# A diffusion transformer layer on one core: the modulation weights streamed at longer intervals

## The chip, the cores and the metric

The kernel runs on one core of one Trainium2 chip. A core has a matrix engine (PE, with its weight loads listed apart as PEld), a vector engine (DVE), a scalar engine (ACT), a general engine (POOL) and a sync engine (SP), which here issues transfers from device memory. Each engine works through its own list of instructions in the order in which the program wrote them. The metric is the device time of the whole program in microseconds (us), as a median of several runs.

## The reference

One transformer layer over 256 latent tokens and 256 context tokens of width 2048, all in float32. Cut to what matters here:

```python
mod = silu(c) @ w_ada + b_ada                      # 6 segments of 2048 columns
sh_a, sc_a, gt_a, sh_f, sc_f, gt_f = split(mod, 6)  # segments 0 to 5
h = rms_norm(x, g_attn) * (1 + sc_a) + sh_a        # the same for the context, from c_ctx
o = hybrid_mixer(h, hc)                            # w_in, four groups of heads, w_out
x = x + gt_a * o                                   # segment 2
h = rms_norm(x, g_ffn) * (1 + sc_f) + sh_f         # segments 4 and 3
x = x + gt_f * swiglu(h, w_g, w_u, w_d)            # segment 5; inner width 5632
out = rms_norm(x, g_final)
```

Segments 0 and 1 are needed before any projection. Segment 2 is first read at the residual of the output projection, segments 3 and 4 at the second norm, and segment 5 at the second residual.

## The kernel before

**Weights.** Every weight matrix is streamed once. `stream_w` loads two chunks of 128 rows by 512 columns (512 KB) with one transfer on SP's queue into a tile `raw` (four buffers, line 125). `split` turns each chunk into a pair: ACT rounds it (`whi`, line 137), and DVE subtracts that from the original (`wlo`, line 140). Six buffers of each hold three loads' worth of pairs. `mm3s` multiplies a pair with a pair of activations in three matmuls (lines 160, 161, 163). With 256 tokens, a load feeds twelve matmuls of 512 columns.

**Modulation columns.** Segments 2 to 5 are not done on PE. `ada_block` makes 512 columns of a segment from eight loads of 512 KB from `w_ada`, through the same four `raw` buffers. For each half of a load DVE multiplies by the conditioning value and adds into `ada_acc` (line 346; the first of the sixteen halves is ACT's, line 344). Four transposes on PE (line 351) and a reduction on DVE (line 354) finish the block. Segment 2's first half is loaded earlier, through other buffers; this is not touched.

**The order.** The program writes out the order of its instructions with a small planner, `Side`. It has a clock, `now`, in estimated microseconds of PE. The main line (projections, output projection, feed-forward) calls `side.pump(cost)` after each load's matmuls; `pump` moves the clock on and lets side tasks write their next step when it is due. The `ada_block` tasks stand in one lane, one block at a time. After each load such a task sets its next due time to the last one plus `gap`. `side.finish(tasks)` writes out whatever is left of the tasks. So `gap` decides after how many loads of the main line a load from `w_ada`, with its two DVE instructions, is put into the lists of SP and DVE.

**Stages**, by the trace before: up to 230 us the first norm and most of the projection; 230 to about 500 us the attention of three groups of heads with the rest of the projections; 500 to 612 us the output projection (`w_out`, first three quarters of its rows) beside the fourth group's attention (`diff`); to 650 us the rest of `w_out`, the second norm and the first gate columns; then the feed-forward in three groups of 4, 4 and 3 blocks of 512 inner columns. In a group all gate and up matrices (`ffn_wg`, `ffn_wu`) come first, then the down matrix (`ffn_wd`) over all the output columns. `side.finish(*gate_tasks)` stands ahead of the output projection, `side.finish(*mod_tasks)` behind its first three quarters.

**The gate rows.** `gate_rows(5, res)` turns segment 5's columns into a row on all partitions: a transpose (line 622), a copy on ACT (line 624), a transfer to device memory (line 626) and one back that spreads it (line 628), both on POOL's queue. The row is first read in the second group (line 1045); the first group only copies its sums out (`act.copy`).

Of the kernel before, what the change touches and what calls it, by code (L numbers as in the profile page):

```python
# [87 lines left out]
def hybrid_dit_kernel(ctx: ExitStack, tc: tile.TileContext, a, out):  # L88
# [31 lines left out]
    def acc():  # L120
        return psA.tile([P, 512], F32, name="acc")
# [23 lines left out]
    def stream_w(w, k0, c0, n, keep=None):  # L145
        src = w[k0 * P:(k0 + 2) * P, c0:c0 + n].rearrange("(k p) n -> p k n", p=P)
        return split(stream_raw(src, [P, 2, n]), n, keep)
# [8 lines left out]
    def mm3s(jobs, w_left=False):  # L156


        for dst, l, r, start, stop in jobs:
            pe.matmul(dst, lhsT=l[0], rhs=r[0], start=start, stop=False)  # L160
            pe.matmul(dst, lhsT=l[0 if w_left else 1], rhs=r[1 if w_left else 0], start=False, stop=False)  # L161
        for dst, l, r, start, stop in jobs:
            pe.matmul(dst, lhsT=l[1 if w_left else 0], rhs=r[0 if w_left else 1], start=False, stop=stop)  # L163

    def sub(pair, *sl):
        return pair[0][sl], pair[1][sl]
# [8 lines left out]
    def tsl(t):  # L175
        return slice(t * P, (t + 1) * P)
# [159 lines left out]
    def ada_block(seg, nb, gap, load):  # L336
        c0 = seg * D + nb * 512
        acc_ = stream.tile([P, 512], F32, name="ada_acc", bufs=2)
        for k2 in range(8):
            raw = load(ada_rows[:, 2 * k2:2 * k2 + 2, c0:c0 + 512], [P, 2, 512])  # L340
            for kk in range(2):
                kc = 2 * k2 + kk
                if kc == 0:
                    act.activation(acc_, raw[:, 0, :], AF.Copy, scale=cs[:, 0, 0:1])
                else:
                    dve.scalar_tensor_tensor(out=acc_, in0=raw[:, kk, :], scalar=cs[:, 0, kc:kc + 1], in1=acc_, op0=ALU.mult, op1=ALU.add)  # L346
            due[0] = max(due[0] + gap, side.now - 4 * gap)
            yield 0.0, max(0.0, due[0] - side.now)
        ps = misc()
        for j in range(4):  # L350
            pe.transpose(ps[:, tsl(j)], acc_[:, tsl(j)], ident)
        k4 = slice(4 * nb, 4 * nb + 4)
        base = colA1 if seg == 4 else colA
        dve.tensor_reduce(out=mcol[seg][:, k4], in_=ps.rearrange("p (j n) -> p j n", j=4), axis=AX.X, op=ALU.add)
        dve.tensor_tensor(out=mcol[seg][:, k4], in0=mcol[seg][:, k4], in1=base[:, seg * 16 + 4 * nb:seg * 16 + 4 * nb + 4], op=ALU.add)
        if seg == 4:
            dve.tensor_tensor(out=mcol[4][:, k4], in0=mcol[4][:, k4], in1=colB[:, 16 + 4 * nb:20 + 4 * nb], op=ALU.mult)
        yield 0.3, 0.0

    def add_ada(seg, gap, load, nbs=range(4)):  # L360
        due[0] = side.now
        return [side.add(ada_block(seg, nb, gap, load), lane="gate", width=1) for nb in nbs]
# [256 lines left out]
    def gate_rows(seg, pool_):  # L619

        ps = misc()
        pe.transpose(ps[0:16, 0:P], mcol[seg], ident)
        gr = small.tile([16, P], F32, name="gr", bufs=1)
        act.copy(gr, ps[0:16, 0:P])
        gd = dram.tile([D], F32, name=f"gd{seg}")
        pool.dma_start(gd.rearrange("(n p) -> n p", p=P), gr)
        g = pool_.tile([P, D], F32, name="gate")
        pool.dma_start(g, gd.partition_broadcast(P))
        return g

    GAP = 2.6
    gate_tasks = add_ada(2, GAP, stream_raw, (2, 3))
    mod_tasks = add_ada(4, GAP, stream_raw) + add_ada(3, GAP, stream_raw)

# [359 lines left out]
    def gu(w, fb):  # L994
        accs = [acc() for _ in range(2)]
        for k2 in range(0, KC, 2):
            w_ = stream_w(w, k2, fb * 512, 512)
            mm3s([j for t in range(2) for j in gu_jobs(accs[t], w_, k2, t)])
            side.pump(2.6)
        return accs  # L1000

    def act_T(sg, ps, pair, t):
        dve.tensor_tensor(out=sg, in0=ps, in1=sg, op=ALU.mult)
        yield 0.0, 1.5
        transposes_ff(pair, sg, t)
        yield 0.43, 0.0
# [7 lines left out]
        dve.tensor_tensor(out=pair[1][:, :, tsl(t)], in0=v, in1=pair[0][:, :, tsl(t)].bitcast(F32), op=ALU.subtract)  # L1014

    groups = [(0, 4), (4, 8), (8, 11)]
    gate_f = add_ada(5, 4.0, stream_raw)
    gfin = ff.tile([P, D], F32, name="gfin")
    pool.dma_start(gfin, a["g_final"].partition_broadcast(P))
    for gi, (f0, f1) in enumerate(groups):  # L1020
        last = gi == len(groups) - 1
        aT, tasks = {}, {}
        for fb in range(f0, f1):
            ga = gu(a["ffn_wg"], fb) if fb else first_g
            sg = []
            for t in range(2):
                s_ = ff.tile([P, 512], F32, name="sg", bufs=4)
                act.activation(s_, ga[t], AF.Silu)
                sg.append(s_)
            ua = gu(a["ffn_wu"], fb)  # L1030
            aT[fb] = (ff.tile([P, 4, S], F32R, name="ah", bufs=6), ff.tile([P, 4, S], F32R, name="al", bufs=6))
            tasks[fb] = [side.add(act_T(sg[t], ua[t], aT[fb], t), lane="e", width=4) for t in range(2)]
        if gi == 0:
            side.finish(*gate_f)
            gtf = gate_rows(5, res)
        def down_jobs(ps, w_, fb, j, t):
            return [(ps, sub(aT[fb], slice(None), jj, tsl(t)), w_[jj - j], fb == f0 and jj == 0, fb == f1 - 1 and jj == 3) for jj in (j, j + 1)]

        def down_evac(ps, nb, t):
            c = slice(nb * 512, (nb + 1) * 512)  # L1040
            if gi == 0:
                act.copy(y[nb][:, t, :], ps)
            elif not last:
                dve.tensor_tensor(out=y[nb][:, t, :], in0=ps, in1=y[nb][:, t, :], op=ALU.add)
                dve.tensor_tensor(out=y[nb][:, t, :], in0=y[nb][:, t, :], in1=gtf[:, c], op=ALU.mult)
                dve.tensor_tensor(out=x2[:, t, c], in0=x2[:, t, c], in1=y[nb][:, t, :], op=ALU.add)
            else:
                dve.tensor_tensor(out=y[nb][:, t, :], in0=ps, in1=gtf[:, c], op=ALU.mult)
                dve.tensor_tensor(out=x2[:, t, c], in0=x2[:, t, c], in1=y[nb][:, t, :], op=ALU.add)
                act.activation(y[nb][:, t, :], x2[:, t, c], AF.Square, accum_out=ss3[:, t, nb:nb + 1])  # L1050
                if nb < 3:
                    dve.tensor_tensor(out=x2[:, t, c], in0=x2[:, t, c], in1=gfin[:, c], op=ALU.mult)

        for nb in range(4 - last):
            accs = [acc() for _ in range(2)]
            for fb in range(f0, f1):
                side.finish(*tasks[fb])
                for j in (0, 2):
                    w_ = stream_w(a["ffn_wd"], fb * 4 + j, nb * 512, 512)
                    mm3s([q for t in range(2) for q in down_jobs(accs[t], w_, fb, j, t)])  # L1060
                    side.pump(2.6)
            for t in range(2):
                down_evac(accs[t], nb, t)
# [92 lines left out]
```

## Time and profile before

| | |
|---|---|
| median of 3 runs | 1394.29 us (1393.55 to 1402.66) |
| profiled execution | 1398.19 us |
| its span in the trace | 1396.4 us |
| PE busy | 1356.3 us, 97% |
| weight loads busy (PEld) | 1080.1 us, 77% |
| DVE busy | 913.2 us, 65% |
| ACT busy | 619.1 us, 44% |
| moved from device memory | 310.36 MB, 224 GB/s over the span |

Busy time of PE is modelled: matmuls overlap their successors, so a stretch with short gaps can still read as fully busy. The granted clock of PE was 0.994 of full speed over the span. The 16 DMA engines' busy share is a mean.

### The profile page before, as it was taken

What the parts mean: (1) busy time and instruction counts of PE and PEld (TensorE: products, weight loads), DVE (VectorE), ACT (ScalarE), POOL (GpSimd) and SP (SyncE); (2) the same over time, 40 slices, a digit from 0 to 9 for tenths busy, and PEclk for the clock granted to TensorE, in tenths of its full rate; (3) what the DMA queues carried; (4) which work ended last, traced back from release to release, by engine and by line L of the source; (5) the groups of instructions that cost most, each with busy time, mean ns of one, the idle gap of its engine ahead of it and who ended that gap; (6) DMA issues with size and microseconds to landing.
All of it is one profiled execution on the core that took longest, in us unless ns stands there. A gap on an engine that the chain in (4) does not pass through costs nothing.

```text
span 1396.4 us, 19886 instructions
## 1 busy us (share of the span) xinstructions
PE 1356.3 (97%) x7082; PEld 1080.1 (77%) x7082; DVE 913.2 (65%) x1623; ACT 619.1 (44%) x1180; POOL 34.6 (2%) x46
## 2 busy tenths in 40 slices
PE   6999999999999999999999999999999999999997
PEld 4766778767886687777877788888888888888886
DVE  3555679988887827769667765445455565555575
ACT  4522223455333626548443454444444444444443
POOL 1010000100000000000000000000000000000000
PEclk9999999999999999999999999999999999999999
DMA  9998896667888736455878876666666656666654
GB/s 337 329 313 281 279 314 213 200 223 248 282 257 293 236 102 203 147 159 182 277 270 287 284 257 217 192 196 195 186 190 187 191 176 209 193 192 186 191 173 144
DMA packets 183607, 313.78 MB, mean 225 GB/s; under 512 B 14002, under 2 KB 53972, under 8 KB 182356
## 3 DMA queue, kind: packets, MB, share of 16 engines
q1 hardware_dynamic: 179104, 302.03, 67.8%
q0 software_dynamic: 1056, 7.36, 1.4%
q10 hardware_dynamic: 3348, 3.13, 0.7%
q8 instruction: 55, 0.90, 0.2%
q14 instruction: 44, 0.36, 0.1%
HBM read 310.36 MB, written 2.11 MB: 224 GB/s over the span
## 4 chain that ended last, share of the span: by engine, by line
PE 77%; DMA 11%; DVE 6%; ACT 2%; issue 2%; POOL 0%; ACTq 0%; SPq 0%; POOLq 0%; DVEq 0%
PE acc L160 24%; PE acc L161 23%; PE acc L163 23%; DMA raw<-in_w_ada_dram 5%; PE m L270 2%; DVE wlo L140 2%; DVE ada_acc L346 2%; DMA raw<-in_w_in_dram 2%; DMA araw<-in_w_ada_dram 1%; DMA raw<-in_ffn_wg_dram 1%; DMA raw<-in_ffn_wu_dram 1%; ACT whi L137 1%; PE m L601 1%; PE m L550 1%; PE m L839 1%
## 5 line engine op out<-in xcount | busy, mean ns | idle before, releaser
L140 DVE TENSOR_TENSOR wlo<-raw,whi 128x512 fp32r<-128x512 f32 (+1 forms) x764 | 491.0, 681 | 336.0 <-ACT whi L137 323.0
L137 ACT CAST whi<-raw 128x512 fp32r<-128x512 f32 (+1 forms) x764 | 433.3, 615 | 601.9 <-PE acc L161 398.8
L160 PE MATMUL acc<-whi,h_hi 128*128 128x512 f32 x704 | 276.6, 393 | 4.2 <-ACT whi L137 4.0
L161 PE MATMUL acc<-whi,h_lo 128*128 128x512 f32 x704 | 274.3, 390 | 0.0
L163 PE MATMUL acc<-wlo,h_hi 128*128 128x512 f32 x704 | 191.8, 391 | 1.6 <-DVE wlo L140 1.4
L346 DVE SCALAR_TENSOR_TENSOR ada_acc<-raw,cs,ada_acc 128x512 f32<-128x512 f32 x210 | 156.8, 747 | 37.0 <-DMA raw<-in_w_ada_dram 31.0
L160 PE MATMUL acc<-whi,h 128*128 128x512 f32 (+1 forms) x416 | 167.4, 405 | 2.7 <-DVE ropet L569 1.6
L160 PEld LDWEIGHTS acc<-whi,h_hi 128*128 128x128 f32 x704 | 132.1, 188 | 36.0 <-ACT whi L137 9.5
L161 PE MATMUL acc<-whi,h 128*128 128x512 f32 (+1 forms) x416 | 158.2, 382 | 0.0
L163 PEld LDWEIGHTS acc<-wlo,h_hi 128*128 128x128 f32 x704 | 131.8, 188 | 31.3 <-DVE wlo L140 4.1
L161 PEld LDWEIGHTS acc<-whi,h_lo 128*128 128x128 f32 x704 | 132.2, 188 | 26.7 <-DVE h_lo L956 0.2
L160 PE MATMUL acc<-whi,ah 128*128 128x512 f32 (+1 forms) x364 | 138.9, 383 | 0.0
L161 PE MATMUL acc<-whi,al 128*128 128x512 f32 (+1 forms) x364 | 138.6, 382 | 0.0
L163 PE MATMUL acc<-wlo,h 128*128 128x512 f32 (+1 forms) x416 | 114.9, 381 | 0.2 <-DVE wlo L140 0.2
L160 PEld LDWEIGHTS acc<-whi,h 128*128 128x128 f32 x416 | 78.4, 189 | 27.6 <-issue 10.5
L163 PE MATMUL acc<-wlo,ah 128*128 128x512 f32 (+1 forms) x364 | 96.2, 382 | 0.0
L163 PEld LDWEIGHTS acc<-wlo,h 128*128 128x128 f32 x416 | 76.6, 189 | 15.7 <-DVE wlo L140 1.2
L161 PEld LDWEIGHTS acc<-whi,h 128*128 128x128 f32 x416 | 78.7, 189 | 12.9 <-issue 1.4
L160 PEld LDWEIGHTS acc<-whi,ah 128*128 128x128 f32 x364 | 68.4, 188 | 13.3
L161 PEld LDWEIGHTS acc<-whi,al 128*128 128x128 f32 x364 | 68.4, 188 | 13.2
L163 PEld LDWEIGHTS acc<-wlo,ah 128*128 128x128 f32 x364 | 67.6, 188 | 13.3
L160 PE MATMUL acc<-whi,o_hi 128*128 128x512 f32 x128 | 51.4, 402 | 0.0
(228 smaller groups left out, 1275.7 us busy)
## 6 DMA issues: line engine op xcount, KB each, us to landing
raw<-in_w_ada_dram SPq DMA_DIRECT2D x112, 512.0 KB, 4.5
raw<-in_ffn_wg_dram SPq DMA_DIRECT2D x88, 512.0 KB, 4.2
raw<-in_ffn_wu_dram SPq DMA_DIRECT2D x88, 512.0 KB, 4.3
raw<-in_ffn_wd_dram SPq DMA_DIRECT2D x88, 512.0 KB, 4.6
raw<-in_w_in_dram SPq DMA_DIRECT2D x72, 512.0 KB, 5.0
araw<-in_w_ada_dram SPq DMA_DIRECT2D x128, 256.0 KB, 4.7
raw<-in_w_out_dram SPq DMA_DIRECT2D x32, 512.0 KB, 3.8
araw<-in_w_ada_dram SPq DMA_DIRECT2D x16, 512.0 KB, 5.4
```

Of the source, the lines that this page charges most:

```text
L137: act.copy(hi, raw[:, k])
L140: dve.tensor_tensor(out=lo, in0=raw[:, k], in1=hi.bitcast(F32), op=ALU.subtract)
L160: pe.matmul(dst, lhsT=l[0], rhs=r[0], start=start, stop=False)
L161: pe.matmul(dst, lhsT=l[0 if w_left else 1], rhs=r[1 if w_left else 0], start=False, stop=False)
L163: pe.matmul(dst, lhsT=l[1 if w_left else 0], rhs=r[0 if w_left else 1], start=False, stop=stop)
L270: pe.matmul(mv[32 * j:32 * j + 32, :P], lhsT=cs32[:, kc, :], rhs=raw[:, kk, j // 2, tsl(j % 2)], start=(kc == 0), stop=(kc == KC - 1), ski ...
L346: dve.scalar_tensor_tensor(out=acc_, in0=raw[:, kk, :], scalar=cs[:, 0, kc:kc + 1], in1=acc_, op0=ALU.mult, op1=ALU.add)
L550: pe.transpose(ps[:, tsl(j)], src[:, tsl(j)], ident)
L601: pe.matmul(o[:, :S], lhsT=vt(kc)[:, v0:v0 + P], rhs=pT[:, kc, :], start=(kc == 0), stop=(kc == 3))
L839: pe.matmul(sc, lhsT=df_qT[hb, h, tsl(t)], rhs=df_kT[h // 2][hb, h % 2, :], start=True, stop=True)
```

## The change

Two intervals grow and one point moves. Segments 2 (second half), 4 and 3, ten blocks with 80 loads, are planned one load per 3.6 units of the planner's clock in place of 2.6. Segment 5, four blocks with 32 loads, is planned one per 8.0 in place of 4.0. The `finish` of segment 5 and its `gate_rows` move from the first group of the feed-forward to the second, to the same place in it: behind the gate and up matrices, ahead of the down matrix.

```diff
-    GAP = 2.6
+    GAP = 3.6
     gate_tasks = add_ada(2, GAP, stream_raw, (2, 3))
     mod_tasks = add_ada(4, GAP, stream_raw) + add_ada(3, GAP, stream_raw)
...
-    gate_f = add_ada(5, 4.0, stream_raw)
+    gate_f = add_ada(5, 8.0, stream_raw)
...
-        if gi == 0:
+        if gi == 1:
             side.finish(*gate_f)
             gtf = gate_rows(5, res)
```

No instruction is added or removed; DVE, ACT and PE have as many of each kind as before. What it does to the order is seen at three places. The numbers behind a tile's name only tell one tile from another.

SP's list at the first up matrix of the feed-forward, before:

```order
L125 DMA raw_6721<-in_ffn_wu_dram 128x2x512
L125 DMA raw_6744<-in_w_ada_dram 128x2x512
L125 DMA raw_6748<-in_ffn_wu_dram 128x2x512
L125 DMA raw_6770<-in_w_ada_dram 128x2x512
L125 DMA raw_6774<-in_ffn_wu_dram 128x2x512
L125 DMA raw_6796<-in_ffn_wu_dram 128x2x512
L125 DMA raw_6818<-in_w_ada_dram 128x2x512
L125 DMA raw_6822<-in_ffn_wu_dram 128x2x512
L125 DMA raw_6844<-in_w_ada_dram 128x2x512
```

The same place now:

```order
L125 DMA raw_6721<-in_ffn_wu_dram 128x2x512
L125 DMA raw_6744<-in_w_ada_dram 128x2x512
L125 DMA raw_6748<-in_ffn_wu_dram 128x2x512
L125 DMA raw_6770<-in_ffn_wu_dram 128x2x512
L125 DMA raw_6792<-in_ffn_wu_dram 128x2x512
L125 DMA raw_6814<-in_w_ada_dram 128x2x512
L125 DMA raw_6818<-in_ffn_wu_dram 128x2x512
L125 DMA raw_6840<-in_ffn_wu_dram 128x2x512
L125 DMA raw_6862<-in_ffn_wu_dram 128x2x512
```

Between the first and the last load of segment 5 stood 44 weight loads in SP's list before, with one or two between neighbours; now it is 94, mostly three between neighbours, and the loads reach through the first group's down matrix into the second group's first gate matrix.

SP's list where the projections end and the output projection begins, before:

```order
L125 DMA raw_5210<-in_w_in_dram 128x2x512
L125 DMA raw_5244<-in_w_in_dram 128x2x512
L125 DMA raw_5316<-in_w_out_dram 128x2x512
L125 DMA raw_5368<-in_w_out_dram 128x2x512
L125 DMA raw_5398<-in_w_out_dram 128x2x512
L125 DMA raw_5420<-in_w_out_dram 128x2x512
```

The same place now:

```order
L125 DMA raw_5157<-in_w_in_dram 128x2x512
L125 DMA raw_5189<-in_w_ada_dram 128x2x512
L125 DMA raw_5241<-in_w_out_dram 128x2x512
L125 DMA raw_5263<-in_w_ada_dram 128x2x512
L125 DMA raw_5297<-in_w_out_dram 128x2x512
L125 DMA raw_5319<-in_w_ada_dram 128x2x512
L125 DMA raw_5331<-in_w_ada_dram 128x2x512
L125 DMA raw_5335<-in_w_out_dram 128x2x512
L125 DMA raw_5357<-in_w_out_dram 128x2x512
```

Before, the last load of the 80 stood five loads ahead of the first `w_out` load. Now 15 of the 80 stand behind it, among 14 of the 24 `w_out` loads of that stage; the other ten have none.

DVE's list in the same stage, behind the first residual (lines 898 and 899; lines 845 to 847 and 859 belong to `diff`), before:

```order
L899 TENSOR_TENSOR x_5286<-x_5286,tm 128x512
L846 TENSOR_SCALAR p<-p,l_5530 128x512
L140 TENSOR_TENSOR wlo<-raw,whi 128x512
L847 SCALAR_TENSOR_TENSOR p<-p,st 128x512
L140 TENSOR_TENSOR wlo<-raw,whi 128x512 x7
L859 TENSOR_REDUCE ss<-ropet 128x2
```

The same place now:

```order
L899 TENSOR_TENSOR x_5211<-x_5211,tm 128x512
L846 TENSOR_SCALAR p<-p,l_5479 128x512
L354 TENSOR_REDUCE mcol_317<-m 128x4
L847 SCALAR_TENSOR_TENSOR p<-p,st 128x512
L355 TENSOR_TENSOR mcol_317<-mcol_317,colA 128x4
L140 TENSOR_TENSOR wlo<-raw,whi 128x512 x4
L346 SCALAR_TENSOR_TENSOR ada_acc<-raw,cs,ada_acc 128x512 x5
L859 TENSOR_REDUCE ss<-ropet 128x2
```

The multiply-adds of the modulation now stand between the weights' subtractions and the softmax work of the fourth group of heads, where there were none.

## Rows read from the trace of the kernel before

**Rows 1.** The page, part 1: busy time, share of the span, count.

```profile
PE 1356.3 (97%) x7082; PEld 1080.1 (77%) x7082; DVE 913.2 (65%) x1623; ACT 619.1 (44%) x1180; POOL 34.6 (2%) x46
```

**Rows 2.** Windows: busy us and instructions of each engine in four stretches.

```profile
core 0: us, PE busy (x) PEld busy (x) DVE busy (x) ACT busy (x) POOL busy (x), PEclk, DMA share, GB/s
230.00:500.00 270.00, 259.00 (x1245) 202.44 (x1244) 225.60 (x444) 118.25 (x260) 12.81 (x12) 0.99 0.74 239
500.00:650.00 150.00, 148.44 (x691) 115.66 (x689) 106.59 (x208) 82.31 (x170) 5.29 (x9) 1.00 0.48 157
650.00:810.00 160.00, 154.00 (x682) 121.56 (x682) 120.13 (x194) 71.86 (x129) 1.39 (x2) 1.00 0.82 274
1000.00:1160.00 160.00, 160.00 (x719) 132.72 (x718) 89.15 (x140) 70.94 (x126) 0.00 (x0) 1.00 0.63 190
```

**Rows 3.** Windows of line 346 alone: DVE busy us (count), the same stretches.

```profile
230.00:500.00 270.00, 111.91 (x150) 0.99 0.74 239
500.00:650.00 150.00, 0.00 (x0) 1.00 0.48 157
650.00:810.00 160.00, 44.90 (x60) 1.00 0.82 274
```

**Rows 4.** Waits of weight loads, 650 to 810 us: total us, times, longest.

```profile
PEld acc L160 <- ACT whi L137: 9.5, 18, 1.8
PEld acc L163 <- DVE wlo L140: 3.8, 7, 1.7
```

**Rows 5.** Waits of SP's queue, 650 to 810 us.

```profile
SPq L125 <- DVE wlo L140: 90.2, 51, 5.8
SPq L125 <- DVE ada_acc L346: 25.1, 31, 2.4
```

**Rows 6.** Waits of DVE, 650 to 810 us.

```profile
DVE ada_acc L346 <- DMA raw<-in_w_ada_dram: 21.1, 16, 4.3
DVE wlo L140 <- ACT whi L137: 13.7, 15, 1.8
```

**Rows 7.** The chain that ended last, 850 to 880 us: start us, us.

```profile
860.33 0.91 PE acc L163 x4
863.04 0.91 PE acc L163 x4
865.76 0.91 PE acc L163 x4
```

**Rows 8.** The page, part 5: busy us, mean ns of one.

```profile
L140 DVE TENSOR_TENSOR wlo<-raw,whi 128x512 fp32r<-128x512 f32 (+1 forms) x764 | 491.0, 681 | 336.0 <-ACT whi L137 323.0
L346 DVE SCALAR_TENSOR_TENSOR ada_acc<-raw,cs,ada_acc 128x512 f32<-128x512 f32 x210 | 156.8, 747 | 37.0 <-DMA raw<-in_w_ada_dram 31.0
```

**Rows 9.** The page, part 6: KB of a load, median us to landing.

```profile
raw<-in_w_ada_dram SPq DMA_DIRECT2D x112, 512.0 KB, 4.5
```

**Rows 10.** Waits of PE's matmuls, 230 to 500 us.

```profile
PE m L607 <- ACT p L579: 1.8, 1, 1.8
PE m L550 <- DVE mcol L355: 1.6, 1, 1.6
PE acc L160 <- DVE ropet L569: 1.6, 1, 1.6
PE m L692 <- ACT p L579: 1.3, 1, 1.3
```

**Rows 11.** Waits of weight loads, 500 to 650 us.

```profile
PEld acc L163 <- DVE wlo L140: 3.4, 8, 1.1
PEld m L839 <- ACT p L579: 1.0, 1, 1.0
```

**Rows 12.** Timeline of POOL, 815 to 850 us: start, us, instruction, idle before.

```profile
836.37 0.51 POOL L626 DMA_DIRECT2D gd<-gr  x1 [166.45 <-ACT gr L624]
839.42 0.55 POOL L628 DMA_DIRECT2D gate<-gd  x1 [2.55 <-DMA gd<-gr]
```

**Rows 13.** Line 628 alone: us to landing of its two transfers.

```profile
DMA to landing us min/median/max: 7.1/7.8/8.6
```

**Rows 14.** Timeline of DVE, 1118 to 1128 us: the gate row's first use.

```profile
1124.06 1.28 DVE L1045 TENSOR_TENSOR y<-y,gate 128x512 f32<-128x512 f32 x2
```

## The prediction

> **What bounds the kernel now.** I read the page's first part first: PE is busy for 97% of the span, DVE for 65%, ACT for 44% [rows 1]. So PE sets the time, and a change that adds and removes no instruction can only win or lose where PE waits. The windows show where that is [rows 2]. From 1000 to 1160 us PE is busy for all 160 us. In the chain that ended last, the fourth matmul group of one load of weights follows that of the load before by 2.72 us (863.04 - 860.33) [rows 7]; this is PE's own pace when nothing stops it, with DVE busy for only 89 of 160 us. Three stretches are short of it: 11.0 us of idle PE from 230 to 500 us, 1.6 us from 500 to 650 us, 6.0 us from 650 to 810 us.
>
> Next, what those stretches have in common. The modulation's multiply-adds (line 346) take 111.9 us of DVE in the first stretch, none in the second and 44.9 us in the third [rows 3]. DVE is busy for 84%, 71% and 75% of them (225.60 of 270, 106.59 of 150, 120.13 of 160). The queue waits of the third stretch tell the mechanism. SP waits 90.2 us for DVE's subtraction and 25.1 us for the multiply-add to free one of the four `raw` buffers [rows 5]; DVE waits 21.1 us for loads of `w_ada` to land and 13.7 us for ACT's rounding [rows 6]; and weight loads of PE wait 9.5 us for the rounding and 3.8 us for the subtraction [rows 4]. A ring of four buffers is turning slower than PE eats.
>
> **Part 1, the feed-forward (interval 4 to 8).** First what is lost there now. From below: 719 matmuls took 160 us undisturbed, 0.2225 us each, so the 682 of the third stretch are worth 151.8 us, and 8.2 us are lost. This is low, since the stretch holds part of the second norm's transposes, which are shorter. From above: the two waits together, 13.3 us, some of which may pass under a running matmul. I take the middle, 10.75 us.
>
> On how to read that loss, the rows give two answers: PE reads 6.0 us idle, while its weight loads read 121.56 us busy against 132.72 us in the undisturbed stretch, which is 13.5 us short when scaled to 160 us [rows 2]. The Trainium skill, in Perfetto Trace Analysis, Identifying the Most-Contended Engine, calls matmul busy time a poor measure and the busy share of weight loads a good one; by it this part would be worth 13.5 us, by matmul busy time 6.0 us. The waits above lie at 13.3 us and the count at 8.2 us, so the trace leans to the page's measure without settling it.
>
> Next, what is left of it. SP's list has 44 weight loads between the first and last of segment 5 before, and 94 now, mostly three to one. Four buffers turn once per four loads. With three weights to one `w_ada`, that is 3 x 2.72 = 8.2 us of PE's time; with the denser pattern before (28 to 44) it is 4 x 44/72 x 2.72 = 6.7 us. A landing takes 4.5 us [rows 9], two multiply-adds 1.5 us and two subtractions 1.3 to 1.4 us [rows 8], 7.3 us if they come one behind the other. So the ring was short by 0.6 us a turn, and now has 0.9 us to spare. DVE's own work per turn is 3 x 1.36 + 1.49 = 5.6 us of the 8.2. The loads now lie under the gate, up and down matrices up to the second group, where DVE had 44% of its time free [rows 2]: two multiply-adds per three loads fill 1.5 of 8.2 us. I leave 0.75 us of waits for blocks' ends (transposes, the first half on ACT) and take a gain of **10 us**, ends 5 and 13.3.
>
> **Part 2, attention (interval 2.6 to 3.6).** Of the 80 loads, 15 are now behind the first load of `w_out`: 30 multiply-adds of 0.747 us, 22.4 us of DVE [rows 8]. From 230 to 500 us DVE falls from 225.6 to 203.2 us, 84% to 75%. What PE waits for there is mostly not weights but the softmax and rope chains: 1.8 and 1.3 us for an exponential before scores, 1.6 us for a modulation column, 1.6 us for a rope [rows 10]. These chains pass through DVE's list, behind the multiply-adds, so a shorter list brings them forward. No row shows this stretch at 75%. I take a slope from its neighbour, which has the same kind of work: 4.1 us of idle PE per 100 us at 84%, 1.0 us at 71%, so 0.24 per point. Nine points over 270 us are a gain of **6 us**. Ends: 0, if the chains wait on ACT and PE alone, and 11.0, all the idle there is.
>
> **Part 3, the output projection.** The same 22.4 us arrive in the second stretch: 106.6 becomes 129.0 of 150 us, 86%. By the same slope 15 points over 150 us cost **5 us**. Ends: 0, if it fits into DVE's 43 idle us, and 22.4 us, every moved instruction exposed. I stay low because PE has a lead there: pairs for three loads, and with `diff` between them a load takes PE longer than 2.72 us. Weight loads already wait 3.4 us for subtractions in that stretch [rows 11], so it is not free. Segments 3 and 4 are still done ahead of the second norm: the last of their loads stands before 18 loads of `w_out`.
>
> **Part 4, the gate row.** Its chain moves from the first group's down matrix to the second's, and so loses its long slack. Before, from the start of its first transfer to the latest landing of its second it took 839.42 + 8.6 - 836.37 = 11.7 us [rows 12, 13]. Its first reader comes eight loads behind the same place in the program, 8 x 2.72 = 21.8 us; in the trace that reader started at 1124.06 us [rows 14]. So 10 us of cover are left, and I cost it at **nothing**. If the transfers queued as badly as to double, DVE would wait 2 us, in front of the subtractions of the next weights. POOL has nothing else queued behind it but the last norms.
>
> **Sum.** -10 - 6 + 5 + 0 = -11 us. The profiled execution took 1398.19 us, so it would be about 1387 us; it is 3.9 us above the median of 1394.29 us, which I use for the forecast: **1383 us**, 0.8% faster.
>
> **The rivals.** A change of 1% (14 us, below 1380.3 or above 1408.2 us) is about what a measurement of this kernel can tell from none.
>
> *Both relieved.* If PE's lead covers the output projection's extra work whole (part 3 at about 1) and attention gains 8, with 11 in the feed-forward, the sum is -18: 1376 us. For it: the second stretch has 43 us of idle DVE; in attention the busy measure hides short gaps, as it does in the third stretch (6.0 read, 8.2 to 13.3 lost). Against it: 86% is more than attention has now, and that loses 4%.
>
> *A toll per load.* Each `w_ada` load might cost PE the same wherever it stands: it takes one of four buffers and two DVE slots ahead of the next weight. Then the feed-forward's 10.75 us, 0.34 us for each of 32 loads, are spread and not removed, and parts 2 and 3 cancel: about -2, 1392 us. For it: SP waits on buffers all through [rows 5]. Against it: a stall needs the ring to run dry, and three pairs in hand (8.2 us) outlast one landing of 4.5 us. The Trainium skill's Perfetto Trace Analysis, Roofline, bears on this rival: it puts a single core's ceiling at 16 transfer engines' 435 GB/s, far above the 274 GB/s of that stretch, so by it bandwidth was not scarce and spacing the loads frees none.
>
> *The output projection becomes DVE's.* The fourth group's softmax, the subtractions and the multiply-adds share one list in order. If that list falls behind for good, the moved 22.4 us show almost whole: +20 there, -6 in attention, -10 in the feed-forward: +4, 1398 us. It decides for slower once a moved microsecond costs more than 0.7 (16 of 22.4). For it: the multiply-adds come in runs of up to five there, 3.7 us ahead of a `diff` reduction. Against it: attention at 84% lost 11 us of 270 with 112 us of them.
>
> *It does not do what it says.* Were the loads bunched at a `finish`, PE would stand still; the order shows none there, so this is worth 2%, about 1396 us.
>
> **Chances.** Forecast (1380 to 1388) 0.42; both relieved 0.33; toll 0.15; output projection 0.08; bunched or a late gate row 0.02. The forecast's own range is 1378 to 1388 us. The range for 8 in 10 takes in most of both neighbours: 1372 to 1393 us. Faster by over 1% gets the whole of "both relieved" and the low edge of the forecast, 0.39; slower by over 1% needs more than the output projection's case, 0.03; the rest, 0.58, is within 1%.
>
> **What would show it.** Right: in the feed-forward's first gate and up matrices after, weight loads wait under 2 us in place of 13.3, PE's matmuls come at 2.72 us a load, and DVE's wait for landings of `w_ada` is near zero. In attention the waits for exponentials shrink; from 500 to 650 us DVE is busy for some 129 us and weight loads wait longer than 3.4 us for subtractions. The gate row's reader waits for PE, not for a landing. Wrong: waits of the same size in the feed-forward spread over twice the length (toll); a PE idle of 10 us or more between 500 and 650 us (output projection); a wait for `gate` in the second group.

## The result, and the profile after

The change made the kernel slower: 1412.36 us (median of 6 runs, 1408.12 to 1414.63) against 1395.84 us before on the same chip (6 runs, 1392.59 to 1402.66), a ratio of 1.011 with a 95% interval of 1.0085 to 1.0135. The forecast was 1383 us, at most 1393. Single executions of one kernel lie up to 0.5% to either side of its median, and each stage below is read from one execution. Pairs of kernels whose lists are the same up to the feed-forward, or in it, show how far such a reading can be trusted (the labels are those of the experiments): 4.3 us apart at the end of attention (before_ordered, hold_26), 2.5 us in the output projection (gap_only, after), 4.7 us in the first gate and up matrices (before, gap_only), 3.9 us in the first down matrix (after, gate_only).

First the head of the page of after: span, and busy time of each engine. It answers to [rows 1].

```profile
span 1411.3 us, 19892 instructions
PE 1358.8 (96%) x7082; PEld 1080.9 (77%) x7082; DVE 909.5 (64%) x1623; ACT 618.3 (44%) x1180; POOL 34.6 (2%) x46
```

The work is the same; 15 us of waiting came in. Where, the windows of after tell; the first three and the last answer to [rows 2].

```profile
core 0: us, PE busy (x) PEld busy (x) DVE busy (x) ACT busy (x) POOL busy (x), PEclk, DMA share, GB/s
230.00:500.00 270.00, 257.35 (x1247) 202.66 (x1246) 205.57 (x412) 117.14 (x259) 12.17 (x12) 1.00 0.66 207
500.00:650.00 150.00, 141.12 (x647) 108.81 (x646) 116.03 (x220) 74.97 (x152) 5.89 (x8) 0.98 0.64 209
650.00:810.00 160.00, 158.54 (x714) 129.16 (x713) 107.87 (x181) 79.04 (x147) 1.44 (x2) 1.00 0.70 230
820.00:980.00 160.00, 153.00 (x658) 121.04 (x658) 92.69 (x150) 67.88 (x121) 0.00 (x0) 1.00 0.70 228
1000.00:1160.00 160.00, 160.00 (x720) 132.62 (x719) 85.38 (x134) 72.66 (x129) 1.06 (x2) 1.00 0.66 196
...
```

The first gate and up matrices gained (158.54 us of PE against 154.00), attention did not (257.35 against 259.00), the output projection lost (141.12 against 148.44). A stretch that was full before, 820 to 980 us, has 153.00 of 160 us: the first down matrix. Fixed windows cut through stages that shift, so the table gives each stage's length, from its first matmul to the next stage's, read from PE's timeline ("attention" from 230 us).

| us | attention | output projection, norm | first gate, up | first down | second gate, up |
|---|---|---|---|---|---|
| before | 299.9 | 113.5 | 192.2 | 88.1 | 176.8 |
| after | 297.8 | 125.3 | 183.9 | 99.5 | 178.7 |
| difference | -2.1 | +11.8 | -8.3 | +11.4 | +1.9 |

They sum to +14.7 us, the spans' difference being 14.9. Attention's -2.1 us lies within the spread just named; the three large differences lie outside it. The page's costliest groups name a suspect; the last numbers are the engine's idle time ahead of these instructions, and what ended most of it. The second row answers to the one of line 346 in [rows 8].

```profile
L140 DVE TENSOR_TENSOR wlo<-raw,whi 128x512 fp32r<-128x512 f32 (+1 forms) x764 | 487.9, 680 | 236.7 <-ACT whi L137 225.7
...
L346 DVE SCALAR_TENSOR_TENSOR ada_acc<-raw,cs,ada_acc 128x512 f32<-128x512 f32 x210 | 157.2, 749 | 155.5 <-DMA raw<-in_w_ada_dram 138.3
```

DVE stood still for 138.3 us until a load of `w_ada` landed, 31.0 us before. The forecast had this wait near zero. By stretch, DVE's waits in attention, in the first gate and up matrices (with [rows 6] before) and around the first down matrix:

```profile
DVE ada_acc L346 <- DMA raw<-in_w_ada_dram: 34.7, 28, 3.5
```

```profile
DVE ada_acc L346 <- DMA raw<-in_w_ada_dram: 41.8, 14, 4.4
DVE wlo L140 <- ACT whi L137: 5.6, 4, 2.8
```

```profile
DVE ada_acc L346 <- DMA raw<-in_w_ada_dram: 43.1, 12, 5.0
```

Before, the same wait in attention was 9.9 us, and around the first down matrix, where no `w_ada` load stood, none. Now the first down matrix close up. DVE's timeline of after, each row a run of like instructions, in brackets the idle time before it and what ended that:

```profile
865.61 1.54 DVE L346 SCALAR_TENSOR_TENSOR ada_acc<-raw,cs,ada_acc 128x512 f32<-128x512 f32 x2 [4.96 <-DMA raw<-in_w_ada_dram]
867.07 3.69 DVE L140 TENSOR_TENSOR wlo<-raw,whi 128x512 fp32r<-128x512 f32 x6
874.86 1.54 DVE L346 SCALAR_TENSOR_TENSOR ada_acc<-raw,cs,ada_acc 128x512 f32<-128x512 f32 x2 [4.09 <-DMA raw<-in_w_ada_dram]
876.31 3.70 DVE L140 TENSOR_TENSOR wlo<-raw,whi 128x512 fp32r<-128x512 f32 x6
...
893.96 0.75 DVE L346 SCALAR_TENSOR_TENSOR ada_acc<-raw,cs,ada_acc 128x512 f32<-128x512 f32 x1 [4.93 <-DMA raw<-in_w_ada_dram]
```

SP's timeline of the same place, its issues of loads:

```profile
869.59 0.37 SPq L125 DMA_DIRECT2D raw<-in_w_ada_dram  x1
870.79 7.21 SPq L125 DMA_DIRECT2D raw<-in_ffn_wd_dram  x3
878.83 0.37 SPq L125 DMA_DIRECT2D raw<-in_w_ada_dram  x1
880.04 6.98 SPq L125 DMA_DIRECT2D raw<-in_ffn_wd_dram  x3
```

A load of `w_ada` is issued at 869.59 us. DVE comes to its multiply-adds at 870.76 (867.07 + 3.69) and stands there to 874.86, when it lands. Then six subtractions of three loads follow without a pause: two of those loads had been issued before that of `w_ada`, and ACT had rounded both by 874.4 us (it began at 871.16 and 873.24 us). Only these subtractions free their buffers for SP's next loads. So the ring turns in (893.96 - 865.61)/3 = 9.45 us; PE needs 3 x 2.72 = 8.16 us for its three loads. ACT, starved in turn, waits for the down matrix, and PE's weight loads for the subtraction (both 830 to 960 us):

```profile
ACT whi L137 <- DMA raw<-in_ffn_wd_dram: 51.1, 24, 4.4
```

```profile
PEld acc L163 <- DVE wlo L140: 14.4, 20, 1.7
```

DVE's list as built says why. The numbers behind `raw` grow in the order in which the loads are issued; 8472 is a load of `w_ada`, the others are of the down matrix.

```
L140 TENSOR_TENSOR wlo_8414<-raw_8406,whi_8412 128x512
L346 SCALAR_TENSOR_TENSOR ada_acc_7957<-raw_8472,cs_113,ada_acc_7957 128x512 x2
L140 TENSOR_TENSOR wlo_8432<-raw_8428,whi_8430 128x512
L140 TENSOR_TENSOR wlo_8436<-raw_8428,whi_8434 128x512
L140 TENSOR_TENSOR wlo_8454<-raw_8450,whi_8452 128x512
L140 TENSOR_TENSOR wlo_8458<-raw_8450,whi_8456 128x512
```

The multiply-adds of 8472 stand ahead of the subtractions of 8428 and 8450, which were loaded before. In the program's text they come behind: SP's list of loads is in the text's order, DVE's is not. So what the opening section says of the engines' lists, that they are in the order in which the program wrote them, does not hold for DVE. Counted over the lists, a `w_ada` load overtakes at least one older load of weights 25 times of 112 before (8 ahead of the first load of `w_out`, 17 in the feed-forward) and 78 times of 112 after (42 ahead of the first load of `w_out`, 5 among those of `w_out`, 31 in the feed-forward, there by 1.6 loads in the mean against 0.6).

### The profile page after: what moved, and what is told of

It reads as the page before. It is cut to its first block, busy times and chain, and to the rows that moved or that the text cites. A ratio compares the mean times of both kernels' runs of the same rounds, so it can differ in the third digit from the quotient of the medians.

```text
span 1411.3 us, 19892 instructions
## 1 busy us (share of the span) xinstructions
PE 1358.8 (96%) x7082; PEld 1080.9 (77%) x7082; DVE 909.5 (64%) x1623; ACT 618.3 (44%) x1180; POOL 34.6 (2%) x46
## 4 chain that ended last, share of the span: by engine, by line
PE 50%; DMA 7%; DVE 6%; issue 1%; ACT 1%; POOL 0%; DVEq 0%; POOLq 0%; ACTq 0%
PE acc L163 16%; PE acc L160 16%; PE acc L161 16%; DVE wlo L140 3%; DMA raw<-in_w_ada_dram 3%; DMA raw<-in_ffn_wg_dram 2%; DMA raw<-in_ffn_wd_dram 1%; DMA raw<-in_w_out_dram 1%; DVE ada_acc L346 1%; PE m L1011 1%; PE m L855 0%; DMA raw<-in_ffn_wu_dram 0%; ACT whi L137 0%; DVE tm L898 0%; DVE st L577 0%
## 5 line engine op out<-in xcount | busy, mean ns | idle before, releaser
L346 DVE SCALAR_TENSOR_TENSOR ada_acc<-raw,cs,ada_acc 128x512 f32<-128x512 f32 x210 | 157.2, 749 | 155.5 <-DMA raw<-in_w_ada_dram 138.3
L163 PE MATMUL acc<-wlo,ah 128*128 128x512 f32 (+1 forms) x364 | 99.7, 388 | 6.2 <-DVE wlo L140 5.3
L160 PEld LDWEIGHTS acc<-whi,ah 128*128 128x128 f32 x364 | 68.4, 188 | 13.5
```

## Experiments

The theory that these runs were to test, "order": the intervals are harmless, and the overtakings that came with them cost the time. Its rivals: the ring of four buffers is too short for the new spacing; a `w_ada` load costs what it costs wherever it stands; DVE has too much to do.

**The parts alone.** One kernel has only the interval of 3.6, one only the change to segment 5:

```diff
 gap_only                                       gate_only
-    gate_f = add_ada(5, 8.0, stream_raw)      -    GAP = 3.6
+    gate_f = add_ada(5, 4.0, stream_raw)      +    GAP = 2.6
-        if gi == 1:
+        if gi == 0:
```

> Only the first interval is changed (2.6 to 3.6), the feed-forward stays as before. If the losses of the two parts are independent, attention gains 2 us, the output projection loses 12 us and the feed-forward is as before: 1405 us against 1396. If the loss in the feed-forward of the changed kernel came from a late start of that stage, some of it shows here too and the time is above 1408.

> Only segment 5's interval and its finish are changed (4 to 8, second group). Independent parts: first gate and up matrices 8 us shorter, first down matrix 11 us longer, 2 us at the start of the second group: about 1401 us. If the down matrix loses only because the output projection came late, it loses nothing here and the time is 1388.

The first took 1402.61 us (ratio 1.0047, 1.0025 to 1.0068), the second 1402.08 us (1.0034, 1.0014 to 1.0053). Both parts lose, 6.0 and 5.5 us against 1396.62 us before in the same runs; together that is 11.5 of the change's 16.5 us, each of these figures being uncertain by some 3 us. The stages (table below) put the loss of the first into the output projection, that of the second into the first down matrix; each takes back some of it in its own stretch. (The profiled executions show less of the losses, spans of 1397.3 and 1398.0 us against 1396.4: they lie 3.5 and 2.3 us below their kernels' medians, that of before 1.6 us above the 1396.62 us.) The wait for landings of `w_ada` is longer in both than before, but it does not go by the number of overtakings alone: 63.8 us with 64 of them in the first, 98.4 us with 39, all but 8 in the feed-forward, in the second.

**The order alone.** SP's list stays as it is after the change. DVE's multiply-adds, and the first half on ACT, are held behind the rounding and the subtraction that were written last before them; `newest` holds these, and `after` is the kernel's own helper for it. The same was done to the kernel before.

```diff
+                with (after(newest["act"], newest["dve"]) if load is stream_raw else ExitStack()):
                     if kc == 0:
                         act.activation(acc_, raw[:, 0, :], AF.Copy, scale=cs[:, 0, 0:1])
                     else:
                         dve.scalar_tensor_tensor(...)
```

> The changed kernel, with each multiply-add of the modulation held behind the newest weight's subtraction in DVE's list; SP's list is the same. Theory order (DVE's list puts the multiply-adds ahead of subtractions of weights that were asked for earlier, so DVE stands still for a landing with landed weights behind it): DVE's wait for landings of w_ada falls from 138 us to under 80, the first down matrix from 99 us to under 93, total 1398 to 1403. Theory ring (one w_ada in four loads fills four buffers with a turn longer than PE's pace, whatever DVE's order): the down matrix stays at 97 us or more and the total within 4 us of 1412.

> The kernel before, with the same hold. In its DVE list the hold removes 25 overtakings but also puts most multiply-adds of attention earlier than the planner had them. Theory order, if only overtaking counts: 1390 to 1396. Theory cover (what counts is how much DVE work stands between the moment a buffer is free and the multiply-add on what is loaded into it): attention worse, DVE's wait for landings from 31 us to over 60, 1400 or more.

After, held: 1390.48 us, ratio 0.9943 (0.9922 to 0.9965), so the slowdown of 1.1% becomes a gain of 0.6%; "order" had forecast only 1398 to 1403 us. Before, held: 1392.62 us, 0.9971 (0.9954 to 0.9989). The group of the multiply-adds on the page of after held:

```profile
L347 DVE SCALAR_TENSOR_TENSOR ada_acc<-raw,cs,ada_acc 128x512 f32<-128x512 f32 x210 | 157.2, 750 | 10.6 <-DMA raw<-in_w_ada_dram 6.3
```

6.3 us of waiting in place of 138.3, with the same loads in the same order on SP and the same work on DVE. In the feed-forward PE's list is the same too, and of ACT's only three first halves of blocks moved, so there the order alone was tested. In attention and the output projection the hold also moved instructions in PE's and ACT's lists; what it gained there may be in part theirs. DVE's timeline in its first down matrix:

```profile
857.42 1.53 DVE L347 SCALAR_TENSOR_TENSOR ada_acc<-raw,cs,ada_acc 128x512 f32<-128x512 f32 x2
858.93 1.29 DVE L140 TENSOR_TENSOR wlo<-raw,whi 128x512 fp32r<-128x512 f32 x2
861.65 1.29 DVE L140 TENSOR_TENSOR wlo<-raw,whi 128x512 fp32r<-128x512 f32 x2 [1.43 <-ACT whi L137]
864.37 1.29 DVE L140 TENSOR_TENSOR wlo<-raw,whi 128x512 fp32r<-128x512 f32 x2 [1.43 <-ACT whi L137]
865.58 0.75 DVE L347 SCALAR_TENSOR_TENSOR ada_acc<-raw,cs,ada_acc 128x512 f32<-128x512 f32 x1
```

The subtractions come at PE's pace, 2.72 us apart, the multiply-adds fit between them without a wait, and the turn is 865.58 - 857.42 = 8.16 us. Its windows:

```profile
230.00:500.00 270.00, 264.28 (x1275) 209.37 (x1275) 206.47 (x412) 119.58 (x261) 9.10 (x12) 0.99 0.64 207
500.00:650.00 150.00, 144.03 (x659) 109.95 (x658) 124.14 (x239) 81.26 (x169) 5.95 (x8) 0.99 0.65 214
650.00:810.00 160.00, 159.75 (x726) 131.67 (x726) 109.96 (x180) 78.64 (x141) 1.45 (x2) 1.00 0.77 250
820.00:980.00 160.00, 160.00 (x719) 132.67 (x718) 98.49 (x153) 73.42 (x131) 0.00 (x0) 1.00 0.73 236
```

Attention and the feed-forward are now better than before; the output projection still has 6 us of idle PE. That remainder is a second cause.

**A fifth buffer.** Room for it comes from two padding tiles. Once with the list held, once on the change as it is (shown is one of the two lines that name the number of buffers):

```diff
-        raw = stream.tile(shape, F32, name="raw", tag="raw", bufs=4)
+        raw = stream.tile(shape, F32, name="raw", tag="raw", bufs=5)
```

> after_ordered with five raw buffers in place of four (two padding tiles left out to make room). If what the output projection still loses (15 us of idle PE against 7 before) comes from loads that are late, idle PE there falls to 9 us or less, total 1384 or less. If it comes from DVE's own work, the total stays within 3 us of after_ordered's 1390.5.

> The change with a fifth buffer for raw (two padding tiles left out for the room) and no hold on the list. As built, its DVE list has no multiply-add of the feed-forward ahead of the subtractions of weights loaded earlier, while in attention and the output projection 35 of 80 still are. Theory that the order costs the time: the first down stage falls from 99.5 us to 88 to 90 us, the first gate and up from 183.9 to 181 to 183 us, the output projection stays at 120 to 126 us; in all 1391 to 1399 us. Rival, that loads of w_ada under the down matrix cost the time through the transfers: the down stage stays above 95 us and the time above 1403 us.

Held: 1384.54 us, 0.9906 (0.9878 to 0.9935), but not for the reason given: the output projection stayed at 123.2 us, and what was gained lies in attention. Not held: 1400.62 us, 1.0026 (1.001 to 1.0043). The second expectation failed for the down stage: 98.4 us, not 88 to 90. Its premise was a miscount. Counted by load, this list has 85 overtakings of 112, more than the change's 78, and in the down stage a `w_ada` load stands ahead of 2.7 older ones in place of 1.7: with one buffer more the list was built with its multiply-adds further ahead. So the pair is a test of order after all. With five buffers in both, the first down matrix takes 88.5 us held and 98.4 us not held. The wait on the page of the one not held:

```profile
L344 DVE SCALAR_TENSOR_TENSOR ada_acc<-raw,cs,ada_acc 128x512 f32<-128x512 f32 x210 | 157.4, 750 | 144.6 <-DMA raw<-in_w_ada_dram 121.1
```

A fifth buffer does not remove the wait, so a ring that is merely too short is not the cause. In attention it helps either way, by 5 to 6 us, not much more than the 4.3 us by which like lists differ there.

**The output projection: how many loads.** The held list with intervals of 2.6 and 3.0 (segment 5 as changed), which leave none and one of the `w_ada` loads behind the first load of `w_out` in place of 15 (by SP's list as built, where 79 and 65 of the 80 lie ahead; the expectation below has 77 and 64):

```diff
-    GAP = 3.6
+    GAP = 2.6        (3.0 in the other)
```

> Hold as in after_ordered, segment 5 at 8 with the finish in the second group, but segments 2, 4 and 3 at 2.6 again. Theory order: with DVE's list held, the longer interval of segment 5 alone is worth what before_ordered still loses in the first gate and up matrices (6 us of idle PE against under 2): 1387 to 1389. Theory ring: three weights to one w_ada is no better than before_ordered: 1392 or more.

> The same at an interval of 3.0: 77 of the 80 loads lie ahead of the output projection in place of 64. If attention and the output projection trade DVE time one for one, 1388 to 1391, as at 2.6 and 3.6. If the output projection pays more for a multiply-add than attention does, idle PE there is 7 to 9 us in place of 15 with attention at 20 to 24, and the time is 1383 to 1387.

1385.82 us, 0.9917 (0.989 to 0.9943), and 1382.5 us, 0.9894 (0.9865 to 0.9923). Both are a little below the ranges that were expected for "order" and for an output projection that pays more for a load than attention does. Both bring the output projection back to 114 us (before 113.5) and keep the feed-forward's gain.

**The output projection: work or loads.** Three kernels, all held at 3.6. The first leaves out every second multiply-add of segments 3 and 4. The second leaves out the multiply-adds of the loads that stand between the output projection's, and keeps the loads; the third leaves out those loads and keeps the multiply-adds, which read one resident tile instead. `in_out` is true from the first load of `w_out` to `side.finish(*mod_tasks)`.

```diff
 hold_half
+                if kk == 1 and seg in (3, 4):
+                    continue
 w_out_noadd
-                    if kc == 0:
+                    if in_out[0] and kc:
+                        pass
+                    elif kc == 0:
 w_out_noload
-            raw = load(ada_rows[:, 2 * k2:2 * k2 + 2, c0:c0 + 512], [P, 2, 512])
+            raw = held if in_out[0] else load(ada_rows[:, 2 * k2:2 * k2 + 2, c0:c0 + 512], [P, 2, 512])
```

> after_ordered, but every second multiply-add of segments 3 and 4 is left out (64 of 150, so the columns are not those of the reference); all loads stay. If the output projection's and attention's remaining losses are DVE's work, idle PE in the output projection falls from 15 us to 8 to 10, in attention from 19 to 12 to 16, total 1378 to 1385. If they come from the loads, both stay, 1389 or more.

> This is the change with the list held (multiply-adds of w_ada stay behind the subtractions of the newest weights), and in the first three quarters of the output projection the 14 or 15 loads of w_ada are still issued and land, but their multiply-adds on DVE are left out. The stretch from the first matmul of the output projection to the first of the feed-forward's first gate took 122.9 us with the held list at 3.6 and 114.1 us at 3.0. Theory that the loads themselves do it (they sit in the four buffers between the loads of w_out, so that weights come late and ACT waits for them, 17.4 us there against none before): the stretch stays at 120 to 125 us, ACT still waits over 8 us for landings of w_out. Theory that DVE's work or its place in the list does it: 113 to 116 us and no such wait.

> The same kernel as the change with the list held, but in the first three quarters of the output projection the w_ada loads are left out and the multiply-adds, all still there, read one tile that is already in memory. Theory that the loads do it: the stretch falls from 122.9 us to 113 to 116 us, ACT's wait for landings of w_out goes from 17.4 us to under 3. Theory that DVE's work or its place does it: 120 us or more stays, with PE waiting for p or mcol of DVE.

1389.35 us (ratio 0.9939, 0.9917 to 0.9961), 1392.5 us (0.9968, 0.9953 to 0.9983) and 1384.51 us (0.9911, 0.9893 to 0.9929). With half or none of the multiply-adds there the stage stays at 124.9 and 125.8 us; without the loads it falls from 122.9 to 117.0 us, a little short of the 113 to 116 expected. (Its attention ends 3.7 us later than after_ordered's, which is within the spread of like lists.) ACT's wait for landings of `w_out`, 500 to 612 us, in after held, in the kernel without the multiply-adds, and what ACT waits for most in the one without the loads:

```profile
ACT whi L137 <- DMA raw<-in_w_out_dram: 17.4, 6, 5.2
```

```profile
ACT whi L135 <- DMA raw<-in_w_out_dram: 17.3, 4, 9.5
```

```profile
ACT whi L135 <- PE acc L159: 26.4, 14, 4.3
```

Without the loads, and before, ACT has no wait for `w_out` and waits for PE instead, which is as it should be. So the loads of `w_ada` among those of `w_out` cost some 6 of the 9 us by which the held stage is longer than before, give or take the spread of 2.5 us, and the work of DVE alone is not seen to cost any. (PE's granted clock has a part in these lengths; see the last section.) In the kernel without the multiply-adds one path can be followed. ACT's timeline, then PE's:

```profile
540.85 1.14 ACT L135 CAST whi<-raw 128x512 fp32r<-128x512 f32 x2 [9.51 <-DMA raw<-in_w_out_dram]
542.41 0.72 ACT L346 ACTIVATE ada_acc<-raw,cs 128x512 f32<-128x512 f32 x1 [0.43 <-DMA raw<-in_w_ada_dram]
543.04 1.05 ACT L555 COPY pT<-m 128x512 f32<-128x512 f32 x2
```

```profile
533.75 0.71 PE L552 MATMUL m<-ident,p 128*128 128x128 f32 x5
...
543.66 2.56 PE L841 MATMUL m<-df_kT,qT 64*128 64x512 f32 x4 [5.40 <-ACT pT L555]
```

ACT stood 9.51 us for a load of `w_out`, with the copies for `diff` (line 555) behind it in its list, though PE had finished the transposes that they copy by 534.5 us; PE stood 5.40 us for the copies. It is the same fault on another engine: ready work behind an instruction that waits for a landing.

**The fastest tried.** Interval 3.0, held, five buffers:

> The held list at interval 3.0 with a fifth buffer, the candidate for the fastest. At 3.6 the fifth buffer shortened attention from 291.9 to 289.5 us and the output projection from 122.9 to 121.8 us. If buffers limit attention here too: attention 292 to 295 us in place of 296.2 us, 1378 to 1382 us. If not: 1382 to 1384 us, as with four.

1382.03 us, 0.9889 (0.9869 to 0.9909). Attention took 292.2 us in place of 296.4, the output projection 112.7 in place of 114.1, the first gate and up 182.6 in place of 180.7. That is not to be told from hold_30 with four buffers; both beat the kernel before and the change. (For the 289.5 and 121.8 us that the expectation quotes for five buffers at 3.6, the trace has 286.5 and 123.2, and for 291.9 and 296.2 it has 291.7 and 296.4.)

The stages of the profiled executions, us, with the time that DVE waited for landings of `w_ada`:

| | attention | output projection, norm | first gate, up | first down | second gate, up | wait |
|---|---|---|---|---|---|---|
| gap_only | 296.2 | 122.8 | 187.5 | 88.1 | 176.8 | 63.8 |
| gate_only | 299.1 | 113.5 | 185.6 | 95.6 | 178.0 | 98.4 |
| after_ordered | 291.7 | 122.9 | 180.8 | 88.4 | 177.3 | 6.3 |
| before_ordered | 300.9 | 113.6 | 186.5 | 88.1 | 176.8 | 7.9 |
| hold36_raw5 | 286.5 | 123.2 | 182.7 | 88.5 | 177.3 | 2.5 |
| after_raw5 | 291.9 | 119.3 | 186.6 | 98.4 | 178.0 | 121.1 |
| hold_26 | 296.6 | 113.7 | 180.7 | 88.4 | 177.3 | 6.5 |
| hold_30 | 296.4 | 114.1 | 180.7 | 88.4 | 177.3 | 7.5 |
| hold_half | 289.8 | 124.9 | 180.7 | 88.4 | 177.3 | 15.6 |
| w_out_noadd | 291.1 | 125.8 | 180.7 | 88.4 | 177.3 | 2.3 |
| w_out_noload | 295.4 | 117.0 | 180.7 | 88.4 | 177.3 | 3.9 |
| hold30_raw5 | 292.2 | 112.7 | 182.6 | 88.5 | 177.3 | 2.8 |

## Why the prediction was wrong

By stages the sum came out some 26 us too low: 15 us in part 1, 4 in part 2, 7 in part 3.

**The step that failed** is the ring turn of part 1: "Four buffers turn once per four loads ... 7.3 us if they come one behind the other. So the ring was short by 0.6 us a turn, and now has 0.9 us to spare." The loads' spacing was read from SP's list, and DVE's instructions were taken to stand in the same order. They do not. With a multiply-add ahead of two older loads' subtractions, the landing of the youngest load is added to the turn while older loads lie landed behind it: 9.45 us measured, where 7.3 had been worked out and PE allows 8.16. The rows to see it were there. DVE's 21.1 us of waits for landings of `w_ada` [rows 6] were read as a ring that runs dry; before_ordered shows that the overtakings made most of that wait (over the whole program 7.9 us in place of 31.0, and a median 4.0 us lower). A smaller slip in the same step: SP's list has 46 weight loads to the 32 of segment 5 before, and 93 after, not 44 to 28 and 94; the turn that PE allowed before was 4 x 46/78 x 2.72 = 6.4 us, not 6.7.

**Part 1.** The gain in the first gate and up matrices came, 8.3 us of the 10 (3.6 us against gap_only, whose feed-forward has the list of before and took 187.5 us there); "right" signs came only in part, as weight loads waited 4.0 us for subtractions (650 to 810 us), not under 2. But the loads that moved under the down matrix, costed at nothing because "DVE had 44% of its time free", cost 11.4 us there and 1.9 in the second group. DVE was free, and stood waiting. With the order held the first gate and up take 11.4 us less than before, and the two stages behind 0.8 us more, close to the 10 us forecast. That is in part luck: against before_ordered, which has the hold and the old interval, it is 5.7 us, near the low end of the forecast's 5 to 13.3. On the measure of the loss, the 11.4 us lie nearer to the 13.5 us that weight loads' busy time gave than to the 6.0 of matmuls' (the first is what the Trainium skill, Perfetto Trace Analysis, Identifying the Most-Contended Engine, calls the good measure; here the trace agrees).

**Part 2.** -2.1 us in place of -6: DVE's busy share fell to 76% as worked out, but its wait for landings rose from 9.9 to 34.7 us. With a spread of 4.3 us there, one execution does not tell -2.1 from -6. Held, attention gained 8.2 us.

**Part 3.** +11.8 us in place of +5. Held, +9.4. The cause was misplaced as well: the price was worked out from DVE's busy share, but the share read only 77% (116.03 of 150 us, forecast 86%), and taking the work away gave nothing back. It is the loads. Some 6 us of the held stage's 9.4 are shown to be theirs; how a `w_ada` load delays those of `w_out` is not settled, since a fifth buffer cut ACT's wait to 11.8 us (527 to 612 us) without shortening the stage.

**Part 4.** Right: the gate row's first reader, at 1138.9 us, waited neither for the row nor for a landing.

**The rivals.** "The output projection becomes DVE's" had the right sign and, by the stages, a loss over 10 us in the right place (in the window that it named PE was idle for 8.9 us, not 10), for a reason that the runs refute. "A toll per load" is refuted for the feed-forward: held, the ten loads under the first down matrix cost 0.3 us (88.4 against 88.1). In the output projection loads did have a price, 5.9 us for 15 of them or 0.4 us each, near the 0.34 us of this rival; but it is not the same wherever they stand. The argument against it from the ceiling held: after held moves 236 GB/s from 820 to 980 us with PE full, after 228 GB/s with PE short. "Both relieved" failed by the output projection, which PE's lead did not cover; and no load was bunched at a `finish`. None of the rivals had the order in DVE's list.

## What to carry to other kernels

A change to when loads are issued also changes where their consumers stand in the other engines' lists, and a busy share tells nothing of that. Before costing a moved load, follow one turn of the buffer ring through the consumer's list, and ask of each instruction that reads a fresh load which landed work stands behind it; if there is any, add the landing to the turn. Tie the late consumer to the newest older one, and the intervals can be judged for themselves.

## What was not expected of the hardware

Idle time of PE cost more than its length. In the output projection of after, the granted clock fell behind a gap: the windows there, PEclk being the third number from the end.

```profile
556.00:562.00 6.00, 1.75 (x9) 1.54 (x10) 5.46 (x13) 2.40 (x7) 0.00 (x0) 0.81 0.34 111
562.00:566.00 4.00, 4.00 (x10) 3.04 (x10) 3.89 (x6) 0.57 (x1) 0.00 (x0) 0.50 0.58 181
```

The gap before it, on PE's timeline:

```profile
555.98 0.63 PE L550 MATMUL m<-ident,p 128*128 128x128 f32 x4 [0.57 <-DVE p L847]
560.86 1.09 PE L550 MATMUL m<-ident,p 128*128 128x128 f32 x4 [4.25 <-DVE mcol L355]
```

After 4.25 us of standing still PE worked from 562 to 566 us at 0.50 of full speed, that is 1.2 GHz: 10 matmuls in 4 us where 719 in 160 us make 18. PE had been at its full clock up to the gap, and the engine that it waited for was DVE, at work in its list's order.

This bears on the lengths of the output projection. From 500 to 650 us the granted clock reads 1.00 before, 0.98 in after and 0.99 in after_ordered (windows above), and in the kernels without the multiply-adds and without the loads:

```profile
500.00:650.00 150.00, 141.17 (x646) 108.57 (x645) 103.72 (x204) 79.29 (x163) 5.23 (x8) 0.97 0.64 213
500.00:650.00 150.00, 146.20 (x682) 112.98 (x680) 127.57 (x245) 83.80 (x172) 6.71 (x9) 1.00 0.52 169
```

By an estimate from these means (0.01 of 150 us is 1.5 us) the lower clock made up 3 us of the stage in after, 1.5 us in after_ordered, 4.5 us without the multiply-adds and nothing without the loads. Less that, after_ordered and the kernel without the multiply-adds come to 121.4 and 121.3 us, so leaving that work out still gains nothing; and of the 5.9 us that the loads cost, 1.5 us came by way of the clock, behind gaps that are gone without them.
